# Layer 1 mixer: the first four queries projected ahead of values and gates, the other four and the compressed branch inside the attention's first units

## The chip, the cores and the metric

The kernel runs on one core of one Trainium2 chip. The metric is the device time of one execution in microseconds (us). Five engines work side by side and meet through semaphores: TensorE (PE in the profile, its weight loads PEld) does matrix products into PSUM banks, VectorE (DVE) and ScalarE (ACT) do elementwise work, GpSimd (POOL) does almost nothing here, and SyncE (SP) issues the DMAs that move data between memory, SBUF and the tiles.

## The reference, cut to what matters

A trunk of two layers works on one sequence of 256 tokens of width 1024, in float32. Each layer is a half-weighted SwiGLU feed-forward block, a mixer and a second such block, each with a modulated RMS norm in front. The mixer of layer 1, which the change touches, is a native sparse attention:

```
u = h @ in_w
q, kc, vc, ks, vs, kw, vw, gl = split(u)
q_rope = rope_partial(q, pos)
kcmp = compress(kc)
vcmp = compress(vc)
gates = sigmoid(gl)
o_c = softmax(q @ kcmp) @ vcmp
o_s = softmax(q_rope @ rope(ks)) @ vs
o_w = softmax(q_rope @ rope(kw)) @ vw
y = gates[0] * o_c + gates[1] * o_s + gates[2] * o_w
out = y @ out_w
```

There are 16 heads of width 64 in two groups that share keys and values. compress() adds a position table to 15 overlapping blocks of 32 tokens, and puts them through a hidden layer of width 128 with a tanh Gelu. With 256 tokens the selected branch (at most 16 blocks of 64) and the window branch (512) both come out as plain causal attention with keys and values of their own.

## The kernel before, in words

Every float32 product that needs full accuracy is done as three fp32r matmuls: operands are split into a high part and a low rest, and `mm3` adds high x high, high x low and low x high. Weights come as a stream of 128x1024 pieces (512 KB). `Stream.need(i)` takes the next piece: ScalarE copies it to its high part `wh` (line 86), VectorE subtracts to get the low part `wl` (line 90). Seven raw pieces and seven split pieces can be in flight; `free(i)` gives a split piece back after its last matmul. The pieces of the mixer are counted from p0: 0 to 3 compressed and plain keys, 4 and 5 queries 0 and 1, 6 to 8 values and gates, 9 to 14 queries 2 to 7, 15 to 22 the output projection. A "query i" here is a pair of heads, one of each group, 128 columns.

Work is issued through a planner that gives each engine a fixed order from the order of the program and its own estimate of durations. Inside `in_order()` the order of the program holds for TensorE, VectorE and ScalarE; inside the attention of layer 1 it holds for TensorE alone (`tc.manual_schedule`), so VectorE, ScalarE and the DMA queue of SP are ordered by the planner there.

`mixer1` (line 989 on) does this in program order:

- After the norm: key projections in `transition`, then queries 0 and 1 side by side (`proj2`). A query's bank is one of two PSUM tiles `oa`; `do_q` (line 1017) lets ScalarE copy it to `qf` (line 1018), and after every fourth query two DMAs gather its rotary rows to `zq`.
- Four copies of keys (L1031 to L1033), DMAs that gather the rotary rows of the plain keys (L1041), then values and gates (three pieces, 48 matmuls into two banks), a sigmoid for the gates, copies of the values.
- `rope` of the keys, four DMAs back into `kf` (L1064), high and low parts of the keys `kh` and `kl` (L1067 to L1070), and the inputs of the compression `x2` (8 additions, L1081).
- Queries 2 and 3, with the 64 small matmuls of the compression's hidden layer between their steps (`hidden`), a Gelu after each.
- `rope_q(0)`, `stack_q(0, ...)` and `place_q(0, ...)`: the rotated first four queries are split and put into the stacked tile `qs[0]`, high parts in one half of the partitions and low parts in the other. `place_q` takes four DMAs.
- Query 4, the compressed keys (`kbd`), query 5, the compressed scores of the first four queries (`cmp_scores`, 8 products for each of two halves, then `cmp_soft`, a softmax on VectorE and ScalarE), the compressed values (`vb4`).
- The attention. Its unit u (of ten) handles query u: two score sets (one for each group, two branches in each), the softmax of each, transposes of the probabilities of the unit before, and products with values for the unit two before; at the end of the latter the output tile of query u - 2 is finished and split to `yh` and `yl`. Between these, `filler(u, f)` is called four times in a unit: it runs the entries of `sides` and pieces of the output projection (`HalvedProj.some`).

`HalvedProj` has 64 steps of three matmuls; `some(n)` does up to n of those that may run, and 52 of them can run before the last query's tile is needed. In units 2 to 7 it does up to 4 in a unit, from unit 8 on up to 3 in a call. The ScalarE tables change at `preload` (line 210) and at the sigmoid of the gates (L1057): sigmoid, then Gelu, then Exp.

Of the kernel before, what the change touches and what calls it, by code (L numbers as in the profile page):

```python
# [16 lines left out]
P = 128  # L17
# [100 lines left out]
def hybrid_trunk_kernel(ctx: ExitStack, tc: tile.TileContext, xT, c, wst, mst, prm_d, cst_d, wab_d, cw1_d, cw2_d,  # L118
# [656 lines left out]
    class HalvedProj:  # L775
# [213 lines left out]
    def mixer1(prev):  # L989
# [32 lines left out]
        with tc.tile_pool(name="cmp", bufs=1) as cp:  # L1022
            cw1 = cp.tile([P, 2, 16, P], F32, name="cw1")
            nc.sync.dma_start(out=cw1, in_=cw1_d)
            m = cp.tile([P, 4, S], F32, name="m")
            sb = cp.tile([P, 4], F32, name="sb")
            kc = cp.tile([P, 2, S], F32, name="kc")
            b0, b1 = oa(), oa()
            proj2(p0 + 4, p0 + 5, b0[:, 0:S], b1[:, 0:S])
            for q in range(4):  # L1030
                V.tensor_tensor(out=m[:, q], in0=banks[q][:, 0:S], in1=rbs, op=ALU.mult)  # L1031
                V.tensor_copy(out=sb[:, q:q + 1], in_=banks[q][:, S:S + 1])
                A.activation(out=kc[:, q] if q < 2 else kf[:, q - 2], in_=m[:, q], func=ACTF.Identity,  # L1033
                             bias=sb[:, q:q + 1])
# [9 lines left out]
            vb = [ps(), ps()]  # L1044
            for q in range(3):
                wh, wl = st.need(p0 + 6 + q)
                for k in range(3 * q, min(3 * q + 3, KD)):
                    sl = slice((k - 3 * q) * 304, (k - 3 * q) * 304 + 304)
                    for t in range(2):
                        ts = slice(t * P, (t + 1) * P)  # L1050
                        o = vb[t][:, 0:304]
                        mm(o, HH[:, k, ts], wh[:, sl], k == 0)
                        mm(o, HH[:, k, ts], wl[:, sl], False)
                        mm(o, HL[:, k, ts], wh[:, sl], False, k == KD - 1)
                st.free(p0 + 6 + q)
            for t in range(2):
                A.activation(out=gts[:, t], in_=vb[t][:, 256:304], func=ACTF.Sigmoid)  # L1057
                A.activation(out=vp[:, t].rearrange("p a d -> p (a d)"), in_=vb[t][:, 0:256], func=ACTF.Copy)
            preload(ACTF.Gelu_apprx_tanh, gts[:, 1, 0:1])
# [5 lines left out]
            for g in range(2):  # L1065
                a, b = slice(64 * g, 64 * g + 64), slice(64 - 64 * g, 128 - 64 * g)
                A.activation(out=kh[a, g], in_=kf[a], func=ACTF.Copy)  # L1067
                A.activation(out=kh[b, g], in_=kf[a], func=ACTF.Copy)
                V.tensor_tensor(out=kl[a, g], in0=kf[a], in1=kh[a, g].bitcast(F32), op=ALU.subtract)
                V.tensor_tensor(out=kl[b, g], in0=kf[a], in1=kh[a, g].bitcast(F32), op=ALU.subtract)  # L1070
            x2 = []
            for w in range(2):
                t = cp.tile([P, 16, 2, 15], F32, name=f"x2{w}")
                pos = PR("pos")[:, 16 * w:16 * w + 16]
                for half in range(2):
                    rows = slice(64 * half, 64 * half + 64)
                    for g in range(2):
                        a = (kc if g == half else kx)[rows, w]
                        src = bass.AP(tensor=a.tensor, offset=a.offset + half,
                                      ap=[list(a.ap[0]), [2, 16], [16, 15]])  # L1080
                        V.tensor_tensor(out=t[rows, :, g, :], in0=src,  # L1081
                                        in1=pos[rows].unsqueeze(2).to_broadcast([64, 16, 15]), op=ALU.add)
                x2.append(t)
            hb = [ps(), ps()]

            def hidden(w, q):
                o = hb[w][:, 0:32].rearrange("p (g c) -> p g c", g=2)[:, :, 0:15]
                for n in (2 * q, 2 * q + 1):
                    mm(o, cw1[:, w, n], x2[w][:, n], n == 0, n == 15)

            for w in range(2):
# [4 lines left out]
                A.activation(out=hid[w][:, :, 0:15], in_=o, func=ACTF.Gelu_apprx_tanh)  # L1096
            preload(ACTF.Exp, hid[1][:, 0, 0:1])

        ap_ = tc.tile_pool(name="att1", bufs=2)
# [68 lines left out]
        bk = ps()  # L1168
        mm(bk[:, 0:32], cw2[:, 0], hid[0].rearrange("p g c -> p (g c)"), True, True)
        for g in range(2):  # L1170
            rows, cols = slice(64 * g, 64 * g + 64), slice(16 * g, 16 * g + 16)
            A.activation(out=kbd[rows, cols], in_=bk[rows, cols], func=ACTF.Copy)
        hid4 = ap.tile([P, 4, 32], F32, name="hid4", bufs=1)
        V.tensor_copy(out=hid4, in_=hid[1].rearrange("p g c -> p (g c)").unsqueeze(1).to_broadcast([P, 4, 32]))
        b = oa()
        proj(p0 + 12, b[:, 0:S])
        do_q(5, b[:, 0:S])
        for i in range(4):
            cmp_scores(i)
        sc0 = cmp_soft(0)  # L1180
        bv = ps()
        mm(bv[:, 0:P], hid4.rearrange("p a c -> p (a c)"), cw2[:, 1], True, True)
        V.tensor_tensor(out=vb4, in0=bv[:, 0:P].unsqueeze(1).to_broadcast([P, 4, P]),
                        in1=C("vsel").rearrange("p (a d) -> p a d", a=4), op=ALU.mult)
        late = {}

        def q_step(i, k):
            if k == 0:
# [5 lines left out]
                st.free(p0 + 7 + i)  # L1194
                do_q(i, b)

        def q7(k):
            q_step(7, k)

        def soft1():  # L1200
            late["sc"] = cmp_soft(1)

        def cmp_second():
            for i in range(4, 8):
                cmp_scores(i)
            soft1()

        def y_tiles(k):
            if k >= 4:
# [6 lines left out]
        for i in range(8):  # L1216
            for g in range(2):
                for br in range(2):
# [29 lines left out]
        sides = {(0, 0): [lambda k=k: q_step(6, k) for k in range(KD)] + [lambda k=k: q7(k) for k in range(2)],  # L1248
                 (0, 1): [lambda k=k: q7(k) for k in range(2, 5)], (0, 2): [lambda k=k: q7(k) for k in range(5, KD)],
                 (0, 3): [lambda: cmp_trans(0, sc0)], (1, 0): [cmp_second],  # L1250
                 (1, 1): [lambda: late.update(z=rope_q(1)), lambda: stack_q(1, 0, 2)],
                 (1, 2): [lambda: stack_q(1, 2, 4), lambda: place_q(1, late["z"])],
                 (2, 0): [lambda: cmp_trans(1, late["sc"])]}
# [140 lines left out]
def _layout(i):  # L1394
# [16 lines left out]
    p_m1 = [_cols(kc)[0], _cols(vc)[0], _cols(ks)[0], _cols(kw)[0]] + qt[:2] + list(tp) + qt[2:] + _halves(ow)  # L1411
# [47 lines left out]
```

## Time and profile before

| | |
|---|---|
| time, median of 3 runs | 1039.91 us (1039.69 to 1040.43) |
| the profiled execution | 1039.33 us |
| its span in the profile | 1037.5 us |
| TensorE busy | 991.4 us, 96% of the span |
| VectorE busy | 813.9 us, 78% |
| ScalarE busy | 564.9 us, 54% |
| mixer of layer 1 | about 697 to 836 us of the span |
| first score matmul of its attention | 752.22 us |

The span is the time from the first to the last record of the profile; the rest of the execution's time lies around it. Times in the rows are microseconds from the span's start, unless ns is said. A row of the timeline has the start, the duration, the engine, the line, the operation with its output and inputs, and in brackets an idle time before it with what ended it. Matmuls overlap in the pipeline, so the cost of one in a stream is the distance between two starts, not its duration. The granted clock is a share of 2.4 GHz; 0.5 is the lower level of 1.2 GHz.

### The profile page before, as it was taken

How to read it: one execution, taken by the hardware profiler on the slowest of the kernel's cores; microseconds unless marked ns; L12 is line 12 of the kernel's file. 1: busy time of each engine (PE TensorE's matmuls, PEld its weight loads, DVE VectorE, ACT ScalarE, POOL GpSimd, SP SyncE). 2: the span in 40 equal slices, each digit the busy share in tenths (PEclk: the TensorE clock that was granted, in tenths of full speed). 3: DMA queues.
4: the chain of work that ended last, by engine and by line, in shares of the span. 5: the costliest groups of instructions: out<-in, count | busy, mean ns of one | idle time of the engine just before them, and what ended most of it. 6: DMA issues, size and time to landing. Idle time of an engine off the chain costs nothing. (4 is left out here: it accounts for less than half of the span.)

```text
span 1037.5 us, 20549 instructions
## 1 busy us (share of the span) xinstructions
PE 991.4 (96%) x8070; PEld 962.1 (93%) x8070; DVE 813.9 (78%) x1552; ACT 564.9 (54%) x972; POOL 1.0 (0%) x13
## 2 busy tenths in 40 slices
PE   3999999999899999999999999999889999999996
PEld 2899999999789999999999999999878899999996
DVE  8979887889776988887789888859888578655554
ACT  5364343566976744444574444457767566444442
POOL 0000000000000000000000000000000000000000
PEclk9999999999999999999999999999989999999999
DMA  9979999957553599998439999962620117766611
GB/s 353 342 272 401 330 330 330 342 178 245 206 199 143 206 383 334 324 346 314 143 125 390 331 331 336 346 212 77 222 86 35 62 62 271 257 220 209 217 65 42
DMA packets 69795, 249.49 MB, mean 240 GB/s; under 512 B 8001, under 2 KB 9793, under 8 KB 69442
## 3 DMA queue, kind: packets, MB, share of 16 engines
q1 hardware_dynamic: 69410, 247.65, 67.2%
q8 instruction: 63, 1.03, 0.4%
q10 hardware_dynamic: 288, 0.52, 0.1%
q14 instruction: 34, 0.28, 0.1%
HBM read 245.39 MB, written 1.05 MB: 238 GB/s over the span
## 5 line engine op out<-in xcount | busy, mean ns | idle before, releaser
L90 DVE TENSOR_TENSOR wl<-raw,wh 128x1024 fp32r<-128x1024 f32 (+1 forms) x339 | 383.7, 1147 | 118.2 <-ACT wh L86 117.4
L86 ACT ACTIVATE wh<-raw 128x1024 fp32r<-128x1024 f32 x315 | 328.2, 1056 | 215.6 <-PE ps L152 104.0
L152 PE MATMUL ps<-HL,wh 128*128 128x256 f32 (+1 forms) x1392 | 392.1, 282 | 2.7 <-DVE HL L438 2.7
L152 PE MATMUL ps<-HH,wh 128*128 128x256 f32 (+1 forms) x1392 | 391.8, 283 | 2.7 <-ACT HH L444 2.7
L152 PE MATMUL ps<-HH,wl 128*128 128x256 f32 (+1 forms) x1392 | 393.4, 283 | 0.8 <-DVE wl L90 0.7
L152 PEld LDWEIGHTS ps<-HH,wh 128*128 128x128 f32 x1392 | 262.8, 189 | 4.2 <-ACT HH L444 3.6
L152 PEld LDWEIGHTS ps<-HH,wl 128*128 128x128 f32 x1392 | 263.9, 190 | 2.0 <-DVE wl L90 2.0
L152 PEld LDWEIGHTS ps<-HL,wh 128*128 128x128 f32 x1392 | 262.6, 189 | 3.4 <-DVE HL L438 3.2
L94 DVE SCALAR_TENSOR_TENSOR junk<-raw,cond 128x1024 bf16<-128x1024 f32 x144 | 175.6, 1219 | 10.4 <-DMA raw<-mst 10.3
L152 PE MATMUL oa<-gl,wh 128*128 128x256 f32 x352 | 98.1, 279 | 0.1
L152 PE MATMUL oa<-gh,wh 128*128 128x256 f32 x352 | 97.9, 280 | 0.1
L152 PE MATMUL ob<-gl,wh 128*128 128x256 f32 x352 | 97.8, 278 | 0.1
L152 PE MATMUL oa<-gh,wl 128*128 128x256 f32 x352 | 97.7, 278 | 0.0
L152 PE MATMUL ob<-gh,wh 128*128 128x256 f32 x352 | 97.7, 278 | 0.0
L152 PE MATMUL ob<-gh,wl 128*128 128x256 f32 x352 | 97.6, 277 | 0.0
L163 ACT ACTIVATE gh<-g 128x256 fp32r<-128x256 f32 x82 | 33.5, 417 | 73.1 <-DVE g L472 73.1
L152 PEld LDWEIGHTS oa<-gl,wh 128*128 128x128 f32 x352 | 66.2, 188 | 0.5 <-DVE gl L164 0.5
L152 PEld LDWEIGHTS oa<-gh,wh 128*128 128x128 f32 x352 | 66.2, 189 | 0.5 <-ACT gh L163 0.5
L152 PEld LDWEIGHTS ob<-gl,wh 128*128 128x128 f32 x352 | 66.1, 188 | 0.3 <-DVE gl L164 0.3
L152 PEld LDWEIGHTS oa<-gh,wl 128*128 128x128 f32 x352 | 66.3, 188 | 0.0
L152 PEld LDWEIGHTS ob<-gh,wh 128*128 128x128 f32 x352 | 66.1, 188 | 0.1
L152 PEld LDWEIGHTS ob<-gh,wl 128*128 128x128 f32 x352 | 66.1, 188 | 0.0
(245 smaller groups left out, 1333.0 us busy)
## 6 DMA issues: line engine op xcount, KB each, us to landing
raw<-wst SPq DMA_DIRECT2D x315, 512.0 KB, 5.0
raw<-mst SPq DMA_DIRECT2D x144, 512.0 KB, 5.5
cw<-cw SPq DMA_DIRECT2D x1, 2048.0 KB, 7.7
x<-xT SPq DMA_DIRECT2D x1, 1024.0 KB, 5.5
cst<-cst SPq DMA_DIRECT2D x1, 721.0 KB, 7.1
wab<-wab SPq DMA_DIRECT2D x1, 512.0 KB, 4.2
out<-raw ACTq DMA_DIRECT2D x2, 256.0 KB, 2.0
out<-raw SPq DMA_DIRECT2D x2, 256.0 KB, 2.1
```

The source lines that it names most:

```text
L86: nc.scalar.activation(out=h, in_=raw, func=ACTF.Copy)
L90: nc.vector.tensor_tensor(out=l[:, cols], in0=raw[:, cols], in1=h.bitcast(F32)[:, cols], op=ALU.subtract)
L94: nc.vector.scalar_tensor_tensor(out=self.junk, in0=raw, scalar=1.0, in1=self.cond, op0=ALU.mult, op1=ALU.mult, accum_out=self.modraw[i // ...
L152: PE.matmul(out, lhsT, rhs, start=start, stop=stop, skip_group_check=True)
L163: A.activation(out=h, in_=src, func=ACTF.Copy)
```

## The change

Queries 2 and 3 are projected right after 0 and 1, ahead of the values; the stream's pieces are reordered to match (queries 0 to 3 are pieces 4 to 7, values and gates 8 to 10, queries 4 to 7 pieces 11 to 14). The hidden layer of the compression is woven into the loop over values. The splitting of the keys and the Gelus come after the values in the program. Queries 4 to 7, the compressed keys and values and both halves of the compressed scores become entries of `sides` in units 0 to 3. `some` gets a bound `newest`: in unit u only output tiles up to u - 3 are used. The split of pieces inside the attention follows a table `ahead`.

```diff
-        def some(self, n, last_half=False):
+        def some(self, n, last_half=False, newest=KD):
             while n > 0 and self.todo:
                 h, k, d = self.todo[0]
-                if k == KD - 1 or k not in self.y or h > last_half:
+                if k == KD - 1 or k not in self.y or k > newest or h > last_half:
                     return
...
             do_q(0, b0[:, 0:S])
             do_q(1, b1[:, 0:S])
+            for q in (2, 3):
+                b = oa()
+                proj(p0 + 4 + q, b[:, 0:S])
+                do_q(q, b[:, 0:S])
             zr = rope(zk, cp)
...
+            vb = [ps(), ps()]
+            for q in range(3):
+                wh, wl = st.need(p0 + 8 + q)
...
+                        mm(o, HL[:, k, ts], wh[:, sl], False, k == KD - 1)
+                        hidden(k // 4, 2 * (k % 4) + t)
+                st.free(p0 + 8 + q)
+            for t in range(2):
+                A.activation(out=gts[:, t], in_=vb[t][:, 256:304], func=ACTF.Sigmoid)
+                A.activation(out=vp[:, t].rearrange("p a d -> p (a d)"), in_=vb[t][:, 0:256], func=ACTF.Copy)
+            preload(ACTF.Gelu_apprx_tanh, gts[:, 1, 0:1])
             for w in range(2):
-                b = oa()
-                proj(p0 + 9 + w, b[:, 0:S], [lambda w=w, q=q: hidden(w, q) for q in range(8)])
-                do_q(2 + w, b[:, 0:S])
                 o = hb[w][:, 0:32].rearrange("p (g c) -> p g c", g=2)[:, :, 0:15]
                 A.activation(out=hid[w][:, :, 0:15], in_=o, func=ACTF.Gelu_apprx_tanh)
+            for g in range(2):
...
             preload(ACTF.Exp, hid[1][:, 0, 0:1])
...
-        b = oa()
-        proj(p0 + 11, b[:, 0:S])
-        do_q(4, b[:, 0:S])
...
-        for i in range(4):
-            cmp_scores(i)
-        sc0 = cmp_soft(0)
...
+        sides = {(0, 0): run(4, 0, KD), (0, 1): [cmp_keys] + run(5, 0, 4),
+                 (0, 2): [lambda: cmp_part(0)] + run(5, 4, KD), (0, 3): [cmp_values] + run(6, 0, 4),
+                 (1, 0): run(6, 4, KD), (1, 1): [lambda: cmp_trans(0, late["sc", 0])] + run(7, 0, 4),
+                 (1, 2): run(7, 4, KD), (2, 1): [lambda: cmp_part(1)],
+                 (2, 2): [lambda: late.update(z=rope_q(1)), lambda: stack_q(1, 0, 2)],
+                 (2, 3): [lambda: stack_q(1, 2, 4), lambda: place_q(1, late["z"])],
+                 (3, 1): [lambda: cmp_trans(1, late["sc", 1])]}
+        ahead = {(0, 0): 12, (0, 2): 13, (1, 0): 14, (2, 0): 15, (3, 0): 16, (4, 0): 17, (5, 0): 18, (6, 0): 19, (7, 0): 20,
+                 (8, 0): 21, (8, 2): 22}
 
         def filler(u, f):
+            if (u, f) in ahead:
+                st.need(p0 + ahead[u, f])
             for job in sides.get((u, f), ()):
                 job()
-            if f == 0:
-                st.need(p0 + 14 + (0, 1, 1, 2, 2, 3, 4, 5, 7, 7)[u])
             if u < KD:
-                op.some((0, 1, 2, 1)[f])
+                op.some((1, 1, 2, 1)[f], False, u - 3)
             else:
-                op.some(3, True)
+                op.some(4, True)
 
         banks_for("att1", 3, 1)
+        st.need(p0 + 11)
```

`run(i, k0, k1)` gives the steps k0 to k1 - 1 of the projection of query i (24 matmuls in 8 steps). `cmp_keys` is the product for the compressed keys and its two copies by ScalarE into `kbd`, `cmp_values` the product for the compressed values and VectorE's `vb4`, `cmp_part(w)` the compressed scores and softmax of four queries. `cmp_trans(w, ...)`, as before, is the two transposes of their probabilities.

## Rows read from the trace of the kernel before

**Rows 1.** The page, section 1: busy time, share of the span, instructions.

```profile
PE 991.4 (96%) x8070; PEld 962.1 (93%) x8070; DVE 813.9 (78%) x1552; ACT 564.9 (54%) x972; POOL 1.0 (0%) x13
```

**Rows 2.** Waits of TensorE from 713 to 836: engine, line, releaser, us, times, longest.

```profile
PE ps L152 <- DMA qs<-zl: 3.7, 1, 3.7
PE oa L152 <- DVE yl L164: 2.9, 2, 2.5
```

**Rows 3.** Windows: stretch before the attention, then units 0 to 3.

```profile
core 0: us, PE busy (x) PEld busy (x) DVE busy (x) ACT busy (x) POOL busy (x), PEclk, DMA share, GB/s
...
739.00:752.20 13.20, 9.49 (x80) 9.25 (x80) 10.25 (x21) 10.52 (x19) 0.00 (x0) 0.89 0.56 186
752.20:761.30 9.10, 9.08 (x59) 8.81 (x59) 7.89 (x31) 4.14 (x15) 0.00 (x0) 0.79 0.38 127
761.30:768.00 6.70, 5.34 (x41) 4.64 (x38) 5.92 (x29) 6.36 (x21) 0.00 (x0) 1.00 0.31 94
768.00:779.80 11.80, 8.75 (x53) 7.07 (x54) 10.53 (x47) 8.22 (x30) 0.00 (x0) 0.86 0.19 67
779.80:786.50 6.70, 6.63 (x52) 5.43 (x52) 5.13 (x29) 5.17 (x21) 0.00 (x0) 0.99 0.00 1
```

**Rows 4.** Windows, columns as above: to unit 3's end, and units 4 to 7.

```profile
716.00:740.00 24.00, 23.50 (x191) 23.25 (x190) 22.75 (x38) 19.81 (x32) 0.00 (x0) 1.00 0.57 192
740.00:786.50 46.50, 38.28 (x270) 34.20 (x270) 38.80 (x152) 34.13 (x102) 0.00 (x0) 0.89 0.33 108
786.50:816.10 29.60, 27.15 (x203) 22.44 (x201) 24.06 (x121) 22.66 (x84) 0.00 (x0) 1.00 0.11 37
```

**Rows 5.** The same windows, VectorE's weight splits of line 90 alone.

```profile
core 0: us, DVE busy (x), PEclk, DMA share, GB/s
716.00:740.00 24.00, 13.10 (x13) 1.00 0.57 192
740.00:786.50 46.50, 6.04 (x5) 0.89 0.33 108
786.50:816.10 29.60, 2.45 (x2) 1.00 0.11 37
```

**Rows 6.** Timeline of TensorE: projections, compressed scores, first score matmuls of units 0, 4, 5.

```profile
713.41 0.28 PE L152 MATMUL oa<-HH,wh 128*128 128x256 f32 x1
...
719.18 0.31 PE L152 MATMUL ps<-wh,HH 128*128 128x304 f32 x1
...
746.32 1.86 PE L152 MATMUL ob<-kbd,nqf 128*128 128x32 f32 x16
748.02 0.47 PE L152 MATMUL ps<-cw,hid 128*128 128x128 f32 x2
752.22 0.55 PE L152 MATMUL ps<-kh,qs 128*128 128x256 f32 x1 [3.74 <-DMA qs<-zl]
...
786.48 0.28 PE L152 MATMUL ps<-kh,qs 128*128 128x256 f32 x1
...
794.21 0.28 PE L152 MATMUL ps<-kh,qs 128*128 128x256 f32 x1
```

**Rows 7.** Timeline of ScalarE: query copies, weight copies, table loads.

```profile
720.58 0.63 ACT L1018 ACTIVATE nqf<-oa 128x256 f32<-128x256 f32 x2
721.10 4.85 ACT L86 ACTIVATE wh<-raw 128x1024 fp32r<-128x1024 f32 x5
725.97 1.28 ACT L1057 ACT_TABLE_LOAD   x1
727.26 0.21 ACT L1057 ACTIVATE gts<-ps 128x48 f32<-128x48 f32 x1
...
729.44 0.30 ACT L210 ACTIVATE dummy<-gts,epst 128x1 f32<-128x1 f32 x1
...
739.72 0.39 ACT L1018 ACTIVATE nqf<-oa 128x256 f32<-128x256 f32 x1 [1.44 <-PE oa L152]
...
741.01 1.28 ACT L210 ACT_TABLE_LOAD   x1
```

More of the change, by code (lines that the diff above doesn't have):

```diff
@@ L1043, in mixer1 @@
             do_q(1, b1[:, 0:S])
[L1044 to L1059, printed above, removed]
+            for q in (2, 3):
+                b = oa()
+                proj(p0 + 4 + q, b[:, 0:S])
+                do_q(q, b[:, 0:S])
             zr = rope(zk, cp)
@@ L1064, in mixer1 @@
                     nc.sync.dma_start(out=kf[64 * g:64 * g + 16, w], in_=zr[r:r + 61:4])
[L1065 to L1070, printed above, removed]
             x2 = []
@@ L1089, in hidden @@
                     mm(o, cw1[:, w, n], x2[w][:, n], n == 0, n == 15)
+            vb = [ps(), ps()]
+            for q in range(3):
+                wh, wl = st.need(p0 + 8 + q)
+                for k in range(3 * q, min(3 * q + 3, KD)):
+                    sl = slice((k - 3 * q) * 304, (k - 3 * q) * 304 + 304)
+                    for t in range(2):
+                        ts = slice(t * P, (t + 1) * P)
+                        o = vb[t][:, 0:304]
+                        mm(o, HH[:, k, ts], wh[:, sl], k == 0)
+                        mm(o, HH[:, k, ts], wl[:, sl], False)
+                        mm(o, HL[:, k, ts], wh[:, sl], False, k == KD - 1)
+                        hidden(k // 4, 2 * (k % 4) + t)
+                st.free(p0 + 8 + q)
+            for t in range(2):
+                A.activation(out=gts[:, t], in_=vb[t][:, 256:304], func=ACTF.Sigmoid)
+                A.activation(out=vp[:, t].rearrange("p a d -> p (a d)"), in_=vb[t][:, 0:256], func=ACTF.Copy)
+            preload(ACTF.Gelu_apprx_tanh, gts[:, 1, 0:1])
             for w in range(2):
-                b = oa()
-                proj(p0 + 9 + w, b[:, 0:S], [lambda w=w, q=q: hidden(w, q) for q in range(8)])
-                do_q(2 + w, b[:, 0:S])
                 o = hb[w][:, 0:32].rearrange("p (g c) -> p g c", g=2)[:, :, 0:15]
                 A.activation(out=hid[w][:, :, 0:15], in_=o, func=ACTF.Gelu_apprx_tanh)
+            for g in range(2):
+                a, b = slice(64 * g, 64 * g + 64), slice(64 - 64 * g, 128 - 64 * g)
+                A.activation(out=kh[a, g], in_=kf[a], func=ACTF.Copy)
+                A.activation(out=kh[b, g], in_=kf[a], func=ACTF.Copy)
+                V.tensor_tensor(out=kl[a, g], in0=kf[a], in1=kh[a, g].bitcast(F32), op=ALU.subtract)
+                V.tensor_tensor(out=kl[b, g], in0=kf[a], in1=kh[a, g].bitcast(F32), op=ALU.subtract)
             preload(ACTF.Exp, hid[1][:, 0, 0:1])
@@ L1164, in mixer1, with cmp_keys, cmp_values @@
         place_q(0, zs)
-        b = oa()
-        proj(p0 + 11, b[:, 0:S])
-        do_q(4, b[:, 0:S])
[L1168 to L1172, printed above, removed]
         hid4 = ap.tile([P, 4, 32], F32, name="hid4", bufs=1)
         V.tensor_copy(out=hid4, in_=hid[1].rearrange("p g c -> p (g c)").unsqueeze(1).to_broadcast([P, 4, 32]))
-        b = oa()
-        proj(p0 + 12, b[:, 0:S])
-        do_q(5, b[:, 0:S])
-        for i in range(4):
-            cmp_scores(i)
-        sc0 = cmp_soft(0)
[L1181 to L1184, printed above, removed]
-        late = {}
+        late = {}
+        def cmp_keys():
+            bk = ps()
+            mm(bk[:, 0:32], cw2[:, 0], hid[0].rearrange("p g c -> p (g c)"), True, True)
+            for g in range(2):
+                rows, cols = slice(64 * g, 64 * g + 64), slice(16 * g, 16 * g + 16)
+                A.activation(out=kbd[rows, cols], in_=bk[rows, cols], func=ACTF.Copy)
+        def cmp_values():
+            bv = ps()
+            mm(bv[:, 0:P], hid4.rearrange("p a c -> p (a c)"), cw2[:, 1], True, True)
+            V.tensor_tensor(out=vb4, in0=bv[:, 0:P].unsqueeze(1).to_broadcast([P, 4, P]),
+                            in1=C("vsel").rearrange("p (a d) -> p a d", a=4), op=ALU.mult)
         def q_step(i, k):
@@ L1195, in q_step, with cmp_part @@
                 do_q(i, b)
[L1197 to L1204, printed above, removed]
+        def cmp_part(w):
+            for i in range(4 * w, 4 * w + 4):
                 cmp_scores(i)
-            soft1()
+            late["sc", w] = cmp_soft(w)
         def y_tiles(k):
@@ L1246, in mixer1, with run @@
                                      done=done if last else None))
[L1248 to L1253, printed above, removed]
+        def run(i, k0, k1):
+            return [lambda k=k: q_step(i, k) for k in range(k0, k1)]
+        sides = {(0, 0): run(4, 0, KD), (0, 1): [cmp_keys] + run(5, 0, 4),
[7 more added lines that the diff above has]
+                 (8, 0): 21, (8, 2): 22}
         def filler(u, f):
+            if (u, f) in ahead:
+                st.need(p0 + ahead[u, f])
             for job in sides.get((u, f), ()):
                 job()
-            if f == 0:
-                st.need(p0 + 14 + (0, 1, 1, 2, 2, 3, 4, 5, 7, 7)[u])
             if u < KD:
-                op.some((0, 1, 2, 1)[f])
+                op.some((1, 1, 2, 1)[f], False, u - 3)
             else:
-                op.some(3, True)
+                op.some(4, True)
         banks_for("att1", 3, 1)
+        st.need(p0 + 11)
         with tc.manual_schedule(engines={nc.tensor.engine}):
```

2 lines of the change are left out of this document (1 added, 1 removed).

## The prediction, made before the changed kernel was run

> **What bounds the kernel now.** I read the page first, then the waits of the changed stage, then its windows, then the timelines of the two engines that the windows point to. The page gives TensorE 96% of the span and VectorE 78% [rows 1]: a change can gain only where TensorE stands still or runs slowly, which is almost only inside the layer 1 mixer. The list of TensorE's waits there is led by two: 3.7 us for the DMA that places the rotated queries, and 2.9 us for the low half of the output tiles [rows 2]. The windows show the same by time. From 739 to 752.2 TensorE is busy 9.49 of 13.20 us; after that standstill its mean clock is 0.79 for 9.1 us; unit 1 has 5.34 busy of 6.70; unit 2 has 8.75 of 11.80 with a clock of 0.86; unit 3 is full again [rows 3]. The granted clock has two levels, 1.2 and 2.4 GHz, so a mean of 0.79 costs (1 - 0.79) x 9.1 = 1.9 us and 0.86 costs 1.65 us. Together with the two waits that is some 10 us, nearly all of it before unit 3.
>
> The second thing to see is that VectorE has little room in this stage. It is busy 22.75 of 24.00 us from 716 to 740, 38.80 of 46.50 to the end of unit 3 and 24.06 of 29.60 to the end of unit 7 [rows 4]. Of this, 13.10, 6.04 and 2.45 us are weight splits [rows 5], many of them of pieces that were wanted only much later: the first 13 operations (two pieces are split in halves) are pieces 6 to 16, and piece 16 belongs to the output projection. So TensorE's gaps are worth filling only as far as VectorE (and ScalarE behind it) can deliver earlier what the filled units need.
>
> **The change, part by part.**
>
> *Two queries moved ahead of the values.* Queries 0 and 1 keep TensorE busy from 713.41 to 719.18, 48 matmuls, 0.120 us each, so one projection of 24 costs 2.9 us [rows 6]. Queries 2 and 3 now follow at once, but a projection needs one of two PSUM tiles, and ScalarE empties the first one only from 720.58 [rows 7], after its four key copies, which stay ahead in program order. TensorE waits until about 721.0: 1.8 us that was not there. A gain is excluded; at worst it is 2.5 us, when a split slips in ahead. The hidden layer of the compression moves from these projections into the values loop: the same matmuls, 0.
>
> *Queries 4 and 5, the compressed scores of the first four, and the two small projections leave the stretch before the attention.* That is 2 x 2.9 + 1.70 (746.32 to 748.02) + 0.6 [rows 6]; they reappear inside unit 0, so TensorE's total is unchanged. TensorE reaches its first score at 748.5 - 8.1 + 1.8 = 742.2, instead of 752.22.
>
> *The rotated queries.* Between the ScalarE copy of query 3 at 739.72 [rows 7] and the first score at 752.22 [rows 6] lie a gather (2 DMAs), the rotation (3 VectorE operations and a matmul), a split, and 4 placing DMAs: 12.5 us. Now query 3 leaves TensorE at 721.0 + 5.8 = 726.8, and 12.5 us later it is 739.3, ahead of 742.2: the 3.7 us wait is hidden by the values loop, and the slow clock after it goes. If the cover fails, by VectorE's fuller queue, the ends are 0 and the old 3.7 + 1.9. The DMA count is the same; on SP's queue the gather and the placing DMAs move ahead of some weight loads and stay behind the key DMAs, and since no wait of TensorE names a weight DMA [rows 2], I cost that at 0. Nothing goes to POOL.
>
> *Key splits and activations moved behind the values.* Program order only; the planner still decides for VectorE and ScalarE (only TensorE's order is by hand inside the attention). But ScalarE's sigmoid, Gelu and Exp table loads now stand between the end of the values and the first exp of the attention: 725.97 to 729.74 for the first two and their operations, 0.4 for the two small Gelus (0.21 each, as the gates at 727.26), 1.6 for the Exp load and its dummy (1.28 + 0.30) [rows 7], 5.8 us; before, they lay beside projections. Values end near 741.6, so the first exp can't run before about 747.4, and the copies of the compressed keys queue behind the exps, near 750. TensorE wants them after score, query 4, half of query 5 and the second score, near 748. I expect a wait of about 2 us there; ends 0 and 4.
>
> The trace shows the activation after the load at 725.97 begin at 727.26, 1.29 us later [rows 7]. The Trainium skill (ScalarE: Activation LUTs, What ACT_TABLE_LOAD costs) says some 2.66 us for every switch of set, a drain included; by that the three switches take 4.1 us more and the time would be 1039.4. The trace speaks against it, and the sum goes by the row.
>
> *Unit order and the output projection.* Output tiles now use only tiles finished a unit earlier, which removes the 2.9 us wait and the slow clock after it [rows 2, 3], and shorter ones of the same kind in units 4 to 7. Unit 2 does none, so 4 of the 52 pieces of 3 matmuls move to the end, where nothing hides them: 12 x 0.12 = 1.4 us lost.
>
> **The sum by VectorE.** TensorE's own work from unit 0 to unit 3 is 29.8 us busy [rows 3] + 8.1 moved in - 1.4 moved out - 3.55 slow clock = 33; 742.2 + 33 = 775. VectorE gives a later time. From 716 to the end of unit 3 it did 22.75 + 38.80 = 61.55 us in 70.5 [rows 4], a share of 87%. Without the splits (13.10 + 6.04, rows above) 42.4 remain, all needed before unit 3 ends; of the splits it needs pieces 6 to 16, the 13.10 us that were spent from 716 to 740 before. That is 55.5 us; at the same 87% it takes 63.6, so unit 3 ends at 779.6 instead of 786.48 [rows 6]: **6.9 us gained**. I take 87% because the ends lie on either side: 95% is the share of 716 to 740, 81% that of units 4 to 7 [rows 4]; the new ScalarE chain and the hand-written order hold it from the first, the waits taken out from the second.
>
> Units 4 to 7 then carry splits that were done ahead before: 24.06 - 2.45 [rows 4, 5] + 4 x 1.22 (2.45 for 2) = 26.5 us; at 87% 30.5 instead of 29.6: **0.9 lost**. Unit time before depends on just this: unit 4, from 786.48 to 794.21 with one of the two splits, takes 7.7 us, unit 3 without one 6.7 [rows 3, 6]. With the 1.4 us at the end the sum is 6.9 - 0.9 - 1.4 = 4.6 us. The profiled execution took 1039.33 us (span 1037.5 and 1.83 around it), 0.58 less than the median of the runs, 1039.91; carried to the median the forecast is **1035.3 us**.
>
> **The rivals.**
> 1. *The gaps fill fully.* VectorE reaches its 95%: unit 3 ends at 716 + 58.4 = 774.4, which is TensorE's own bound of about 775; units 4 to 7 take 27.9. Gain 11.5 + 1.7 - 1.4 = 11.8, 1028.1 us. For it: with the waits on fresh output tiles gone VectorE is seldom blocked by TensorE. Against it: the table loads at the start, and unit 2 still holds the second softmax, rotation and query stack at once.
> 2. *No change: the gain is given back.* VectorE holds some 83.5%: 66.5 us to the end of unit 3 (gain 4.0), 31.7 in units 4 to 7 (2.1 lost), 1.4 lost: 1039.4 us. The splits were early work in slack; deferring them into units that had little slack is the mechanism. The case that the planner puts the moved operations where they were before ends here too, as does a standstill of VectorE for once more the three table loads (3 x 1.28 = 3.8, so 1039.1 us), to which I give 0.03 of this case's chance. The rule of the Trainium skill cited above (ScalarE: Activation LUTs, What ACT_TABLE_LOAD costs) would end here.
> 3. *Slower: the compressed keys come late in unit 0.* Their two ScalarE copies stand behind the three table loads, the exps, and, if the planner hoists them, two weight copies of 0.97 us (4.85 for 5, [rows 7]). TensorE's order is fixed there, so it stands still 2 + 1.9 = 3.9 us, and the standstill of 3.7 brought a slow clock that cost 1.9 us [rows 2, 3]. VectorE, with no new scores, loses 3.9 us and half of the 1.9, unit 3 ends at 784.5, and the backlog of splits makes units 4 to 7 go at the 81% of before, 32.7 us. Gain 2.0 - 3.1 - 1.4 = -2.5, 1042.4 us; it decides from a wait of 4 us upwards. The same follows from a placing DMA that lands after 746.
>
> **How the numbers follow.** A measurement of this kernel tells 0.2%, 2.1 us, from no change. Forecast (a VectorE share of 85 to 92%, worked out in the same way 1030.3 to 1037.7) 0.47, rival 1 0.15, rival 2 0.22, rival 3 0.16. Faster is 0.47 + 0.15 = 0.62, same 0.22, slower 0.16. The range reaches into rival 1 and through rival 2, leaving about a tenth out on each side: 1030.0 to 1042.0; the forecast's own range is 1030.3 to 1037.7.
>
> **What would show it.** Right: the first score matmul at 741 to 744 with no wait on the placing DMA; query 2's first matmul some 1.8 us after the last of query 1; no wait of TensorE on the output tiles' low half; VectorE 85 to 92% busy from 716 to the end of unit 3, which falls near 779.6; one split per unit in units 4 to 7, each about 7.6 us. Wrong: a standstill in unit 0 on the key copies or on exps, a clock below 1.0 after it, or units 4 to 7 longer than 8 us. A first score after 746 would overthrow the forecast.

## The result, and the profile of the changed kernel

The changed kernel is slower: 1048.37 us (median of 4 runs, 1047.89 to 1049.93) against 1039.80 for the kernel before (4 runs), a ratio of 1.0088 with an interval of 1.0071 to 1.0106. The forecast was 1035.3 us, the range ended at 1042.0. The profiled execution took 1047.89 us with a span of 1046.1 us, 8.6 us more span than before, so the two traces show the same loss as the medians. Runs of one kernel scatter (31 runs of the kernel before went from 1036.74 to 1042.60 us, at mean granted clocks of 0.989 to 0.994), so a difference between two traces counts here only where the medians bear it out.

Section 1 of the page of the changed kernel answers to [rows 1]:

```profile
PE 994.2 (95%) x8070; PEld 963.5 (92%) x8070; DVE 814.7 (78%) x1552; ACT 565.2 (54%) x973; POOL 1.0 (0%) x13
```

The work is the same, instruction for instruction, but for one more on ScalarE, a fourth table load. TensorE's 2.8 us more, over the same number of matmuls, go with its lower clock (a mean of 0.989 in place of 0.993); the other lost time is standing still. The waits of TensorE from 713 to 860 answer to [rows 2] (engine, line, releaser, us, times, longest):

```profile
PE ps L152 <- DMA qs<-zl: 11.0, 1, 11.0
PE y L152 <- ACT sq L661: 3.2, 4, 0.9
PE y L152 <- DVE sq L659: 2.4, 1, 2.4
...
```

The wait on the low half of the output tiles is gone, as intended. The wait on the DMA that places the rotated queries has not gone: it has grown from 3.7 to 11.0 us. The windows of the changed kernel, cut at the end of the values loop and at the first scores of units 0, 1, 2, 3, 4, and then units 4 to 7, answer to [rows 3, 4]:

```profile
core 0: us, PE busy (x) PEld busy (x) DVE busy (x) ACT busy (x) POOL busy (x), PEclk, DMA share, GB/s
716.00:739.70 23.70, 22.48 (x177) 21.62 (x176) 20.31 (x33) 16.64 (x26) 0.00 (x0) 1.00 0.65 226
739.70:750.80 11.10, 0.07 (x2) 0.04 (x1) 6.84 (x11) 8.40 (x14) 0.00 (x0) 0.70 0.27 106
750.80:763.20 12.40, 12.40 (x89) 12.12 (x90) 7.12 (x30) 6.76 (x23) 0.00 (x0) 0.86 0.26 90
763.20:772.70 9.50, 7.56 (x61) 6.95 (x59) 9.38 (x36) 6.29 (x17) 0.00 (x0) 1.00 0.27 86
772.70:781.70 9.00, 7.88 (x56) 6.22 (x57) 7.26 (x34) 7.82 (x29) 0.00 (x0) 1.00 0.31 102
781.70:794.30 12.60, 10.15 (x53) 8.08 (x53) 9.58 (x44) 6.16 (x24) 0.00 (x0) 0.73 0.06 21
794.30:823.10 28.80, 26.98 (x202) 22.03 (x200) 23.83 (x118) 22.83 (x83) 0.00 (x0) 1.00 0.11 38
```

Two places stand out: the stretch of 11.1 us in which TensorE does next to nothing, and unit 3, which takes 12.6 us at a mean clock of 0.73 where it took 6.7 before. VectorE's splits in the three windows of [rows 5], by the same view of the changed kernel:

```profile
716.00:740.00 24.00, 12.70 (x13) 1.00 0.65 228
740.00:794.30 54.30, 6.11 (x5) 0.84 0.22 77
794.30:823.10 28.80, 2.45 (x2) 1.00 0.11 38
```

They lie where they lay before, 13, 5 and 2: the planner still did them ahead.

The timeline of TensorE in the changed kernel has the first matmul of the queries, then the first place and the second (start, us, operation, and in brackets the idle time before it with its releaser):

```profile
711.65 0.28 PE L152 MATMUL oa<-HH,wh 128*128 128x256 f32 x1
...
719.22 0.39 PE L152 MATMUL oa<-HH,wh 128*128 128x256 f32 x1 [1.06 <-ACT nqf L1018]
...
738.72 0.52 PE L152 MATMUL ps<-x,cw 128*128 128x30 f32 x4
739.08 0.68 PE L152 MATMUL ob<-zq,cst 128*128 128x256 f32 x2
750.79 0.55 PE L152 MATMUL ps<-kh,qs 128*128 128x256 f32 x1 [11.03 <-DMA qs<-zl]
...
785.89 2.82 PE L152 MATMUL y<-sq,nvp 128*64 128x256 f32 x14 [2.44 <-DVE sq L659]
```

The matmul at 739.08 (`ob<-zq,cst`) is the one that the rotation of the queries needs. It runs right behind the last matmuls of the values loop and its hidden layer, though its operand had long been there: SP issued the two gathers of `zq` from 726.07 to 727.75, as SP's own timeline says, and by the trace's list of DMA issues these gathers land 2.9 to 3.3 us after their issue, so by an estimate from these numbers the operand was there by 731.1.

```profile
726.07 1.68 SPq L721 DMA_DIRECT2D zq<-nqf  x2
...
747.50 0.59 SPq L160 DMA_DIRECT2D qs<-zh  x1
...
749.41 0.59 SPq L160 DMA_DIRECT2D qs<-zl  x1
```

ScalarE's timeline says what stood between the rotation, which VectorE finished at 740.67, and the placing DMAs:

```profile
732.40 1.28 ACT L1092 ACT_TABLE_LOAD   x1 [1.02 <-PE ps L152]
...
737.68 1.28 ACT L1087 ACT_TABLE_LOAD   x1
738.98 0.21 ACT L1087 ACTIVATE gts<-ps 128x48 f32<-128x48 f32 x1
...
739.86 1.28 ACT L210 ACT_TABLE_LOAD   x1
...
742.86 1.28 ACT L210 ACT_TABLE_LOAD   x1
744.15 0.29 ACT L210 ACTIVATE dummy<-hid,epst 128x1 f32<-128x1 f32 x1
744.35 0.40 ACT L163 ACTIVATE zh<-rp 128x256 fp32r<-128x256 f32 x1
744.66 2.57 ACT L1109 ACTIVATE qs<-nqf 64x512 fp32r<-64x512 f32 x4
```

So the chain to the first score is: values loop to 739.1; rotation to 740.67; ScalarE's Gelu table, a Gelu, two key copies and the Exp table to 744.35; the high and low part of the rotated queries and four copies to 747.5; four placing DMAs to 750.8.

**Where the time went.** From stage to stage by the timelines of TensorE (before, then after): first score 752.22 and 750.79, 1.4 us earlier, where 10 were forecast; units 0 to 3, 34.3 and 43.5 us, 9.2 lost, of which 6.7 is work that was moved (8.1 in and 1.4 out, at the prediction's prices); units 4 to 7 up to the last score 27.4 and 27.0, 0.4 gained; last score to the first matmul of the stage behind, 22.7 and 24.4, 1.7 lost. The sum is 9.1 us lost at the stage's end (836.64 and 845.71); 0.5 comes back in the rest of the program.

The 1.4 us at the first score are not the change's. Its trace was 1.8 us ahead already at the first matmul of the queries (711.65, against 713.41 in [rows 6]), where both programs have done the same work; over all the kept traces the first matmul of this mixer's keys comes anywhere from 699.0 to 701.5. Counted from the first matmul of the queries, the first score came after 38.8 us before and after 39.1 us in the changed kernel: nothing was gained there, and the stage as a whole lost 10.8 us in these two traces.

### The profile page after: what moved, and what is told of

Read it like the earlier page. It is cut to its first block, busy times and chain, and to the rows that moved or that the text cites. A ratio compares the mean times of both kernels' runs of the same rounds, so it can differ in the third digit from the quotient of the medians.

```text
span 1046.1 us, 20562 instructions
## 1 busy us (share of the span) xinstructions
PE 994.2 (95%) x8070; PEld 963.5 (92%) x8070; DVE 814.7 (78%) x1552; ACT 565.2 (54%) x973; POOL 1.0 (0%) x13
```

## The experiments

Against the forecast two losses were to be explained, 8.6 us at the first score (750.79 in place of 742.2) and 6 us inside units 0 to 3, and a small one at the end.

**1. The rotation early.** Theory: the rotated queries are late because their instructions stand behind the values loop in program order, and because their tiles lie in the attention's pool, whose memory the hidden layer still reads. The edit issues them before the values loop, with tiles of their own:

```diff
+            zs = rope_q(0)
+            stack_q(0, 0, 2)
+            stack_q(0, 2, 4)
+            place_q(0, zs)
             vb = [ps(), ps()]
...
-        qs = [ap.tile([P, 2, 4, S], F32R, name=f"qs{w}", bufs=1) for w in range(2)]
...
-            zs = [ap.tile([P, S], F32R, tag=t, name=t, bufs=1) for t in ("zh", "zl")]
+            zs = [tmp.tile([P, S], F32R, tag="t", name=t, bufs=3) for t in ("zh", "zl")]
```

> The changed kernel with one thing moved: the rotation, stacking and placing of the first four queries are issued ahead of the loop over values, with tiles of their own (in the changed kernel they stand behind it, and their tiles lie in memory that the compression's hidden layer reads until the end of the loop). Theory (the first score waits 11.0 us because that chain starts only when the loop over values ends): the wait shrinks from 11.0 to under 4 us, the first score comes at 742 to 744 instead of 750.8, the slow clock behind it mostly goes, and the time falls by 7 to 10 us, to 1038 to 1041.5. Rival (VectorE's work in units 0 to 3 sets the end, the late start only shows it): the first score comes earlier but unit 3 ends where it did, near 794, and the time falls by less than 3 us.

Measured: 1041.42 us (10 runs), ratio to before 1.0016 [1.0007, 1.0026]; 7.0 us under the changed kernel. The first score came at 744.00:

```profile
PE ps L152 <- DMA qs<-zl: 3.6, 1, 3.6
...
PE y L152 <- DVE sq L659: 2.4, 1, 2.4
```

The theory holds, but for the slow clock, which it had expected to go: unit 0 ran at 0.87 here and at 0.86 in the changed kernel. What is left of the wait has a cause in ScalarE's timeline of this kernel: the high part of the rotated queries ran at 740.26, just behind the gates' sigmoid with its table load (738.86, 1.28 us). Unit 3 still took 12.6 us, so the second loss is a separate one. Order and memory were changed together here; which of them alone would have held the rotation was not tried. One row of the changed kernel speaks for memory: VectorE's first operation of the rotation, at 739.27, waited 0.22 us for a matmul into `ps`, whose result it doesn't read.

**2. ScalarE's tables behind the rotation.** In the changed kernel, Gelu and Exp loads, Gelus and key splits moved behind `place_q`, nothing else.

```diff
-            preload(ACTF.Gelu_apprx_tanh, gts[:, 1, 0:1])
...
-            preload(ACTF.Exp, hid[1][:, 0, 0:1])
...
         place_q(0, zs)
+        preload(ACTF.Gelu_apprx_tanh, gts[:, 1, 0:1])
...
+        preload(ACTF.Exp, hid[1][:, 0, 0:1])
```

> The changed kernel with the Gelu and Exp table loads, the Gelus and the key splits issued behind the rotation of the first four queries instead of ahead of it; the rotation stays behind the loop over values. Theory (of the 11.0 us some 3.5 are ScalarE's loads and key copies that stand between the rotation and its split, the rest is the chain itself): the first score comes near 747, the time falls by 3 to 4 us, to 1044.5 to 1045.5. Rival (the chain waits for memory or DMAs, not for ScalarE): the first score stays within 1 us of 750.8 and the time within 1.5 us of 1048.4.

Measured: 1044.63 us (4 runs), ratio 1.0046 [1.0028, 1.0064]; the first score at 747.27, its wait 7.7 us instead of 11.0. So 3.3 of the 11.0 us are ScalarE's queue; the rest is the chain itself, which starts only behind the values loop.

**3 and 4. The rule for output tiles, alone.** First the changed kernel with the filler's old counts and without the bound on the newest tile:

```diff
-                op.some((1, 1, 2, 1)[f], False, u - 3)
+                op.some((0, 1, 2, 1)[f])
             else:
-                op.some(4, True)
+                op.some(3, True)
```

> The changed kernel with the output projection as before: pieces (0, 1, 2, 1) in a unit from unit 2 on, with the newest tile allowed, 3 in a call from unit 8 on. Theory (the bound on the newest tile saves waits in units 2 to 7 and costs 1.4 us at the end): the wait on the low half of the output tiles is back, units 4 to 7 take 29.5 us or more instead of 28.8, the time rises by 0 to 3 us, to 1048.5 to 1051.5. Rival (the bound is what made the changed kernel slower, by moving pieces to the end): the time falls by 1.4 us or more, to under 1047.

Measured: 1046.22 us (4 runs), 2.1 us under the changed kernel; the stretch from the last score to the first output piece behind the last value matmuls fell back from 14.2 to 12.6 us, and a wait of 0.9 us on `yl` returned. The rule costs, as the rival had it. Then the reverse, the kernel before with the new rule alone:

> The kernel before with the bound on the newest tile alone (pieces (1, 1, 2, 1), tiles up to u - 3, 4 in a call from unit 8 on). Theory: the 2.9 us wait and the slow clock behind it in unit 2 go, 1.4 us come back at the end: 1036 to 1038.5, faster by 1.5 to 4 us. Rival (unit 2 is held by VectorE's softmax, rotation and query stack, so another wait takes the place): within 1 us of 1039.9, or slower by the 1.4 us.

Measured: 1039.45 us (10 runs), ratio 0.9994 [0.9981, 1.0007]: no change, as the rival had it. The wait of 2.9 us on `yl` [rows 2] is gone. The waits of TensorE in this kernel, over the same stretch, begin so:

```profile
PE ps L152 <- DVE csm L1144: 3.8, 1, 3.8
PE y L152 <- ACT sq L661: 2.9, 3, 1.2
PE ob L152 <- DMA zq<-nqf: 1.9, 1, 1.9
PE ps L152 <- DVE sm L645: 1.2, 1, 1.2
```

The first is the old standstill ahead of the first score, put down here to an operation of VectorE that ended at the same moment. The second is the wait of the value matmuls for ScalarE's copies of the transposed probabilities. The same row of the kernel before reads:

```profile
PE y L152 <- ACT sq L661: 0.3, 1, 0.3
```

In the kernel before, an output piece stood between the second transposes of a unit and the value matmuls of the next and covered these copies; with the bound it is missing there. The changed kernel shows the same row with 3.2 us (above). The third row stands in unit 1, ahead of any output piece: there the kernel before waits 1.1 us, and with 1.9 us and a clock of 0.81 in place of 1.00 unit 1 took 2.2 us longer in this execution, which was 1.1 us over the median. Leaving unit 1 aside, the rule gave and took the same: units 2 to 7 up to the last score took 44.3 us in place of 45.9, the stretch from there to the stage behind 24.4 in place of 22.7.

**5. Unit 3.** Theory: in the changed kernel unit 2 holds the second compressed softmax, the second rotation and its own softmax, all on VectorE, and the copy of the last probabilities transposed in unit 2 stands behind them. VectorE's timeline of the changed kernel:

```profile
781.82 0.42 DVE L714 TENSOR_TENSOR rp<-zq,cst 128x256 f32<-128x256 f32 x1
782.15 0.42 DVE L1146 TENSOR_REDUCE csm<-sqs 128x16 f32<-128x256 f32 x1
...
784.22 0.81 DVE L649 TENSOR_SCALAR p<-p,sm 128x256 f32<-128x256 f32 x3
784.93 0.43 DVE L164 TENSOR_TENSOR zl<-rp,zh 128x256 fp32r<-128x256 f32 x1
785.27 0.56 DVE L659 COPY sq<-ps 128x384 f32<-128x384 f32 x1
```

TensorE had begun these transposes at 780.51; their copy came at 785.27, and TensorE, whose order is fixed, waited 2.44 us for it. The edit gives this one copy to ScalarE, on top of experiment 1:

```diff
-if n > 16 and t % 6 == 0:
+if n > 16 and t % 6 == 0 and t != 6:
```

> The kernel of the early rotation (e1_rot_early) with one copy of transposed probabilities, the one of unit 2 that VectorE makes, given to ScalarE. In e1_rot_early unit 3 takes 12.6 us; TensorE waits 2.4 us there for that copy, which stands in VectorE's queue behind the second compressed softmax and the second rotation, and the slow clock follows. Theory (this one copy in VectorE's backlog makes the loss of unit 3): the wait goes, unit 3 takes 8 to 9.5 us, the time falls by 3 to 4.5 us, from 1041.4 to 1037 to 1038.5. Rival (VectorE's backlog as a whole sets unit 3): another wait of over 1.5 us takes its place and the time falls by less than 1.5 us.

Measured: 1038.46 us (10 runs), ratio 0.9989 [0.9980, 0.9999], 3.0 under experiment 1; unit 3 took 8.2 us instead of 12.6. The theory holds.

**6. Experiment 1 with the old output rule**, the edit of experiment 3:

> The kernel of the early rotation (e1_rot_early) with the output projection as before (newest tile allowed, 3 pieces in a call from unit 8 on). Theory (the bound costs what it moves to the end, 1.7 us, and saves next to nothing in units 2 to 7): the time falls by 1.5 to 2.7 us, from 1041.4 to 1038.7 to 1040. Rival (with an earlier start the waits for fresh tiles bite): within 1 us of 1041.4, with a wait on the low half of the output tiles of 1.5 us or more in the list.

Measured: 1040.52 us (10 runs), ratio 1.0009 [0.9996, 1.0021], 0.9 under experiment 1. Less than the theory expected, and the intervals of the two kernels overlap: the old rule gives back the end but brings its own wait of 0.9 us on `yl`, and a wait of 2.2 us in unit 3 stays.

**7. The high part of the rotated queries on VectorE**, so that it does not stand behind the sigmoid, on top of experiment 1:

```diff
-            split(*zs, zr)
+            if w == 0:
+                V.tensor_copy(out=zs[0], in_=zr)
+                V.tensor_tensor(out=zs[1], in0=zr, in1=zs[0].bitcast(F32), op=ALU.subtract)
+            else:
+                split(*zs, zr)
```

> The kernel of the early rotation (e1_rot_early) with the high part of the four rotated queries made by VectorE instead of ScalarE, whose queue has it behind the sigmoid that waits for the end of the loop over values. Theory (the 3.6 us left before the first score are the placing DMAs behind that copy): the wait falls to 1 to 2.5 us, the first score comes at 741.5 to 743 instead of 744.0, and the time falls by 1.2 to 3 us, to 1038.5 to 1040.2. Rival (the loop over values and the key splits set the first score): it stays within 0.7 us of 744.0 and the time within 1 us.

Measured: 1041.12 us (10 runs), ratio 1.0012 [1.0002, 1.0023]; against experiment 1 the same, so the theory had the first score right and the time wrong. The first score came at 741.99, 2.0 us earlier than in experiment 1; 1.0 of them the trace had already at the copy of query 3 (725.42 in place of 726.38), and 1.1 is the wait on the placing DMA, 2.5 us in place of 3.6. The next unit began at 757.0, 0.3 later: unit 0 took 15.0 us in place of 12.7. TensorE's waits show a new one, on the compressed keys, and ScalarE's timeline its cause:

```profile
PE ob L152 <- ACT kbd L1183: 0.9, 1, 0.9
```
```profile
748.88 1.04 ACT L86 ACTIVATE wh<-raw 128x1024 fp32r<-128x1024 f32 x1
...
750.09 0.36 ACT L1183 ACTIVATE kbd<-ps 64x16 f32<-64x16 f32 x2
```

This is the third rival of the prediction in small: a compressed key behind table loads, exps and a weight copy, at 750.09. It explains 0.9 of the 2.3 us; the rest goes with the clock, as the windows of unit 0 show, of experiment 1 and then of this one:

```profile
744.00:756.71 12.71, 12.62 (x88) 12.11 (x89) 9.09 (x33) 9.47 (x27) 0.00 (x0) 0.87 0.61 212
741.99:757.00 15.01, 14.14 (x88) 13.68 (x89) 10.47 (x34) 11.22 (x30) 0.00 (x0) 0.77 0.52 179
```

By their clocks unit 0 lost (1 - 0.87) x 12.7 = 1.7 us there and (1 - 0.77) x 15.0 = 3.5 us here. The traces show no more than that: the execution traced here took 1039.48 us, 1.6 less than the median, and its unit 3 took 10.6 us in place of 12.6.

**8. The second compressed branch one unit later**, on top of experiment 1, which empties unit 2's queue on VectorE in another way than experiment 5:

```diff
-                 (1, 2): run(7, 4, KD), (2, 1): [lambda: cmp_part(1)],
+                 (1, 2): run(7, 4, KD),
...
-                 (3, 1): [lambda: cmp_trans(1, late["sc", 1])]}
+                 (3, 1): [lambda: cmp_part(1)], (4, 1): [lambda: cmp_trans(1, late["sc", 1])]}
```

> The kernel of the early rotation (e1_rot_early) with the second half of the compressed scores and their softmax in unit 3 instead of unit 2, and their transposes in unit 4. Theory (unit 2 gives VectorE the second softmax, rotation and query stack at once, and unit 3 pays): unit 3 takes 8 to 10.5 us instead of 12.6, units 4 and 5 together at most 1.5 us more, the time falls by 1.5 to 4 us, to 1037.5 to 1040. Rival (the work is the same and only moves): the time stays within 1 us of 1041.4.

Measured: 1037.05 us (10 runs), ratio 0.9978 [0.9969, 0.9987], 4.4 under experiment 1 and 2.6 under the kernel before. Unit 2 took 7.1 us, unit 3 9.1, and the wait of 2.4 us was gone.

**9. The same edit on the changed kernel, without experiment 1:**

> The changed kernel with the second compressed scores and softmax moved from unit 2 to unit 3 and their transposes from unit 3 to unit 4, and nothing else: the rotation stays behind the values loop. Theory (two separate losses, the standstill ahead of the first score and the backlog of VectorE in unit 2): the 11 us standstill stays, unit 3 falls from 12.6 to about 9 us, and the time is 3 to 4.5 us under 1048.4, 1044 to 1045.4 us. Rival (the backlog is a consequence of the late start, and the later start leaves VectorE time to recover): under 1.5 us of gain, 1047 us or more.

Measured: 1044.66 us (4 runs), ratio 1.0044 [1.0029, 1.0059], 3.7 us under the changed kernel, with the 11.0 us wait still there and unit 3 at 9.1 us. The two losses are separate and nearly add up: 7.0 and 3.7 of the 11.3 us by which experiment 8 lies under the changed kernel.

**10. Both cures of unit 3 together**, those of experiments 5 and 8:

> The early rotation and the later second compressed branch, and beside them the copy of unit 2's transposed probabilities on ScalarE. Theory (both cures take away the same backlog of VectorE at the end of unit 2, so the second finds nothing left): within 0.7 us of 1037.05. Rival (VectorE's load sets the pace of every unit, so each microsecond taken off it counts): the 3.0 us that the copy gained alone, 1034 us.

Measured: 1036.75 us (7 runs), ratio 0.9965 [0.9955, 0.9976], 0.3 under experiment 8; by the ratios to the kernel before it is some 1.4, with intervals that overlap. Together the two are 4.7 us under experiment 1, where 3.0 and 4.4 would add up to 7.4: they take away largely the same backlog.

**11. The bound on output tiles loosened by one unit** for the third and fourth filler, on top of experiment 8:

```diff
-                op.some((1, 1, 2, 1)[f], False, u - 3)
+                op.some((1, 1, 2, 1)[f], False, u - 3 + (f > 1))
```

> The early rotation and the later second compressed branch as in the run before, and the bound on output tiles loosened by one unit for the third and fourth filler of a unit, so that unit 2 does pieces again. Theory (the 1.4 to 1.7 us at the end are the four pieces that the bound put off): 1 to 1.7 us faster than without it, about 1035.7 us, and the stretch from the last score to the last output piece back near 12.6 us. Rival (the bound costs nothing once unit 3 is full, or the looser one brings back the wait on output tiles): within 0.5 us of 1037.05.

Measured: 1032.35 us (5 runs), ratio to before 0.9932 [0.9919, 0.9944]: 4.7 us under experiment 8, nearly three times what was expected, and 7.7 under the kernel before. The windows of units 2 and 3 of this kernel:

```profile
765.77:773.52 7.75, 7.00 (x49) 5.63 (x50) 6.74 (x34) 7.60 (x29) 0.00 (x0) 1.00 0.38 129
773.52:781.67 8.15, 8.15 (x68) 7.09 (x67) 7.70 (x33) 5.90 (x22) 0.00 (x0) 1.00 0.10 34
```

Unit 3 is full, at full clock. From the first score to the stage behind it took 85.9 us (743.38 to 829.28) instead of 90.9 (744.73 to 835.67): 1.3 less up to the last unit's first score, 1.5 in the last unit, 2.3 from the last score on. The waits of the value matmuls on ScalarE's copies, 2.6 us in experiment 8, are 0.7 here:

```profile
PE ps L152 <- DVE sq L659: 1.2, 1, 1.2
...
PE y L152 <- ACT sq L661: 0.7, 1, 0.7
```

Counted on TensorE's timelines, experiment 8 did exactly 12 matmuls of the output projection, four pieces, in each of units 3 to 6, though the filler asks for five; with the looser bound unit 2 does 9, and units 3 to 6 do 12 each again. So the looser bound lets no more through in a unit. It lets the pieces begin one unit sooner, which takes 9 matmuls (9 x 0.12 = 1.1 us) off the end, and it moves one piece of each unit from the second filler to the fourth, between the unit's second transposes and the value matmuls of the next, where experiment 8 has none. The edit is shown to be worth 4.7 us here. That what goes beyond the 1.1 us comes by that piece fits the rows of the wait on ScalarE's copies (0.3 before, 2.9 in experiment 4, 2.6 and 0.7 here); a kernel that moves the piece alone was not run, and the share of each in the 4.7 us stays open.

## Why the prediction was wrong, point by point

- **The step that failed is the one on the rotated queries**: "12.5 us later it is 739.3, ahead of 742.2: the 3.7 us wait is hidden by the values loop". It took the delay from query 3's copy to the first score as a property of the operations, which starts with the copy, and moved it with the query. But where the chain starts is set by the program: the change left the rotation where it was, behind the values loop, and put ScalarE's Gelu, key copies and Exp load ahead of its split. Query 3's copy on ScalarE came 14.5 us earlier (725.24 in place of 739.72), and its rotation began at 739.08 all the same. From the copy to the first score it took 25.5 us in place of 12.5: 13.8 to the rotation's matmul, of which the gather needs some 6, 1.6 for the rotation, 3.7 in ScalarE's queue, and 6.4 for split, stacking and placing. (The copy lies 1.6 us ahead of the forecast, about the lead that the trace had from the start.) Experiment 1, which moves the instructions too, with tiles of their own, gives 7.0 us back. The bounds, "0 and the old 3.7 + 1.9", were too narrow for the same reason: the old wait was taken as the worst.
- **The overthrow was named**: "A first score after 746 would overthrow the forecast". It came at 750.79.
- **ScalarE's chain of 5.8 us** was seen, but charged to the compressed keys in unit 0, "about 2 us there". It fell on the rotated queries first: experiment 2 puts 3.3 us on it. A wait on the keys appears only where the first score is early, 0.9 us in experiment 7 and 0.2 in experiment 6.
- **The wait of query 2 on its PSUM tile**: 1.8 us forecast, 1.06 measured as idle time. A values matmul ran in the gap, so query 2's first matmul did come 1.9 us after query 1's last (719.22 and 717.29).
- **VectorE at 87%, unit 3's end at 779.6**: VectorE was busy 20.52 + 39.97 = 60.5 us in 78.3 from 716 to the end of unit 3, 77%. The assumed share was an average, and the fault was in the order: VectorE did 19 us of splits in this time where 13.1 were assumed, since the planner kept its splits ahead, and the second compressed softmax and second rotation met in unit 2. Experiments 5 and 8 put that meeting at 3.0 and 4.4 us; "unit 2 still holds the second softmax, rotation and query stack at once" stood in the text only as an argument against the first rival.
- **Units 4 to 7**, forecast 0.9 us longer by deferred splits: 0.8 shorter (28.8 in place of 29.6; 0.4 when cut at the last score, as in the sum below), since only 2 splits were there, as before.
- **The output rule**: the wait of 2.9 us went, the end grew by 1.7 us (1.4 forecast). But the prediction took the wait and its slow clock for time to be had, and experiment 4 shows that the rule by itself is worth nothing: 1.6 us less in units 2 to 7, 1.7 more at the end. With the bound one unit looser the kernel of experiment 8 became 4.7 us faster (experiment 11).
- **The rivals.** The third rival, slower, was given 0.16, with 1042.4 us. Its second condition, "a placing DMA that lands after 746", is what happened, 4.8 us past the point named; its price was 6 us short: it priced that wait at 4 us and unit 3 at no loss of its own. Its first condition, the compressed keys, did not happen in the changed kernel.
- **The table loads.** The switch of table cost what the row of before says: 1.29 to 1.30 us from each of the four loads to the next activation (732.40 to 733.70, 737.68 to 738.98, 739.86 to 741.16, 742.86 to 744.15). The figure of 2.66 us that the Trainium skill gives (ScalarE: Activation LUTs, What ACT_TABLE_LOAD costs) is not what this trace shows, and the loss has another cause.

In sum, by the profiled runs: 8.6 us missed at the first score, 6.1 in units 0 to 3 (43.5 in place of 779.6 - 742.2 = 37.4), 0.3 at the end, and 1.3 better than forecast in units 4 to 7: 13.7 us, the difference between the forecast gain of 4.6 at the stage's end and the loss of 9.1. The first of these is some 10.4 when counted from the first matmul of the queries, whose lead of 1.8 us the sum leaves in.

## What to carry to other kernels

A chain of operations is not moved by moving what feeds it: look at where each of its instructions stands in the program and on each engine, and whose memory its tiles take over, before a measured delay is carried to a new place. A wait that is removed is worth what the next wait leaves of it, so price the removal with the one that comes next, and an average busy share says nothing of a unit in which three queues meet. Here the changed kernel came to 7.7 us under the kernel before, once the rotation went along, one softmax went a unit later and the output pieces were let through a unit sooner. What the second and third of these would bring to the kernel before was not run.

## What the runs showed that was not expected

The clock of TensorE fell some way into the standstill and came back only after the work had begun again. Windows of the changed kernel, in the standstill and at the start of unit 0:

```profile
739.70:745.00 5.30, 0.05 (x1) 0.00 (x0) 2.67 (x6) 5.19 (x10) 0.00 (x0) 0.91 0.45 181
745.00:750.80 5.80, 0.01 (x1) 0.04 (x1) 4.17 (x6) 3.21 (x5) 0.00 (x0) 0.50 0.11 38
750.80:753.00 2.20, 2.20 (x8) 2.01 (x9) 0.99 (x7) 0.65 (x3) 0.00 (x0) 0.50 0.75 251
753.00:756.00 3.00, 3.00 (x23) 3.00 (x22) 1.57 (x8) 1.21 (x6) 0.00 (x0) 0.79 0.03 10
```

The granted clock is 0.50 (1.2 of 2.4 GHz) over the second half of the standstill and the first 2.2 us of unit 0, and 0.79 in the next 3. Over all of unit 0 it is 0.86 after a standstill of 11.0 us; the kernel before has 0.79 over its shorter unit 0 after one of 3.7 us [rows 3], so the longer wait brought no longer slow stretch: (1 - 0.86) x 12.4 = 1.7 us and 1.9 us. In unit 3 a wait of 2.4 us stands beside a mean of 0.73 over 12.6 us, the idle time included; experiment 5, which takes that wait away, makes the unit 4.4 us shorter, 2.0 more than the wait. The trace of experiment 7 has the same wait of 2.44 us with no fall of the clock:

```profile
774.76:785.40 10.64, 7.56 (x53) 5.92 (x53) 9.54 (x44) 5.98 (x23) 0.00 (x0) 1.00 0.07 25
```

That is 2.4 us over the 8.2 of experiment 5 and 1.9 under the 12.6, so the wait costs its own length, and the clock another 2 us where it falls. Why it fell in one trace and not in the other is not shown.
